# The weights' low part read last in each step of a split-precision encoder block

## The chip, the core and the metric

One NeuronCore of a Trainium2 chip runs the whole block as one program. The metric is the device time of one execution in microseconds (us), as the median of several executions. PE is the matrix engine, PEld the loading of its stationary operand, DVE the vector engine, ACT the scalar engine, POOL and SP the two that mostly issue transfers.

## The reference

The block works on `x` of 256 tokens by 2048 channels, in float32. It is a gated feed-forward layer at half weight, then two token mixers side by side (band attention and retention, each with its own gate), then a second gated feed-forward layer, and a final normalisation:

```python
x = x + 0.5 * swiglu_ffn(rmsnorm(x, g1), w1_gate, w1_up, w1_down)
proj = rmsnorm(x, gm) @ w_in                 # 2048 -> 11264 channels
branch_a = chunked_band_attention(...) @ w_out_att
branch_r = (silu(g_r) * chunkwise_retention(...)) @ w_out_ret
merged = sigmoid(gate_a) * branch_a + sigmoid(gate_r) * branch_r
x = x + merged @ w_out
x = x + 0.5 * swiglu_ffn(rmsnorm(x, g2), w2_gate, w2_up, w2_down)
return rmsnorm(x, gf)
# swiglu_ffn(x, wg, wu, wd) = (silu(x @ wg) * (x @ wu)) @ wd, inner width 5632
```

Nearly all of the time goes into products of the 256 rows with weight matrices that are read once.

## The kernel before, in words

**Split products.** Every float32 operand of a large product is held as two tiles of a shorter type: a high part, and a low part that holds the rest. Activations have `ahi` and `alo`, weights `whi` and `wlo`. A product of 128 rows by 128 depths by 512 columns is the sum of three matmuls into one PSUM bank, in `three` (L126): `ahi`·`whi` at L131, `ahi`·`wlo` at L132, `alo`·`whi` at L133. The activation is PE's stationary operand (128x128, loaded on PEld before every matmul) and the weights are the moving operand (128x512).

**Steps.** The program is a list of steps. A step handles one weight tile of 256 depths by 512 columns (`KC` = 2 blocks of 128 depths). A standard step (`standard`, L135) multiplies it with both halves of the 256 tokens, each into a bank of its own (`acc` 0 and 1), so it is 2 x 2 x 3 = 12 matmuls. Its job, a `Gemm`, has 8, 4 or 2 steps for 16, 8 or 4 blocks of depth; 24 jobs have 8 steps, 40 have 4, and 24 have 2, which is 400 standard steps, 176 of them the first or last of their job. A step of a `Strassen` group, which computes two weight matrices at once with seven products in place of eight, multiplies one 256x512 tile with one set of activations: 2 x 3 = 6 matmuls into one bank. There are 23 groups of 28 steps. `weave` mixes standard steps between the pairs of steps of a group.

**What makes the weights ready.** SP issues the transfer of the raw tile (`raw`, five buffers). `split` (L119) makes the two parts: ACT casts `raw` into `hi` (L123) and DVE then subtracts, `lo` = `raw` - `hi` (L124). In a group some of the tiles are sums of weights instead, made on DVE from two kept tiles `z..k` and `z..x` (L538 subtracts, L551 adds); their parts are named `hiz..` and `loz..`. There are four buffers each for `hi` and for `lo`. `prep_upto` lets the preparation of a step's tiles stand up to three steps ahead of its products in the order of ACT and DVE. ACT and DVE also take the sums out of PSUM (for instance L606, L739 and L742 on ACT, L706 on DVE), so the splits stand in line with that work.

**Order.** Each engine works through its instructions in the order in which the program is written out; nothing reorders them. So PE waits at the first matmul that reads a tile until that tile is there. A buffer of `hi` or `lo` is taken again when the last matmul that reads it has ended.

Of the kernel before, what the change touches and what calls it, by code (L numbers as in the profile page):

```python
# [27 lines left out]
KC = 2  # L28
# [44 lines left out]
def block_kernel(ctx: ExitStack, tc: tile.TileContext, x, g1, w1g, w1u, w1d, gm, w_in, rel, woa, wor, wo,  # L73
                 g2, w2g, w2u, w2d, gf, cos, sin, decay, ident, out):
    nc = tc.nc
# [33 lines left out]
    def weights_tile(name):  # L109
        return wpool.tile([P, KC, NB], F32, tag="raw", bufs=RAW_BUFS, name=name)  # L110

    def chunk(w, r0, c0):
        return w[r0 : r0 + KC * P, c0 : c0 + NB].rearrange("(k p) n -> p k n", p=P)

    def fetch(t, w, r0, c0, parts=(slice(0, KC),)):
        for p in parts:
            nc.sync.dma_start(t[:, p, :], chunk(w, r0, c0)[:, p, :])

    def split(raw, name, parts=(slice(0, KC),)):  # L119
        hi = wpool.tile([P, KC, NB], F32R, tag="hi", bufs=SPLIT_BUFS, name=f"hi{name}")  # L120
        lo = wpool.tile([P, KC, NB], F32R, tag="lo", bufs=SPLIT_BUFS, name=f"lo{name}")
        for p in parts:
            nc.scalar.copy(hi[:, p, :], raw[:, p, :])  # L123
            nc.vector.tensor_sub(lo[:, p, :], raw[:, p, :], hi[:, p, :].bitcast(F32))  # L124
        return hi, lo

    def three(acc, a, w, first, last, read_between=False):

        (ahi, alo), (whi, wlo) = a, w
        more = {"skip_group_check": True} if read_between else {}  # L130
        nc.tensor.matmul(acc, ahi, whi, start=first, stop=False, **more)  # L131
        nc.tensor.matmul(acc, ahi, wlo, start=False, stop=False, **more)  # L132
        nc.tensor.matmul(acc, alo, whi, start=False, stop=last, **more)  # L133

    def standard(job, k0):  # L135

        made = {}
        c = len(steps)

        parts = [slice(j, j + 1) for j in range(KC)] if c == 0 else [slice(0, KC)]  # L140

        def load():
            made["raw"] = weights_tile(f"raw{c}")
            fetch(made["raw"], job.w, job.rows[k0], job.col0, parts)

        def prep():
            made["hl"] = split(made.pop("raw"), c, parts)

        def products(only=None):
            if k0 == 0 and only in (None, 0) and not job.seed:  # L150
                open_banks(job)
            hi, lo = made["hl"]
            for part, (t, cs) in enumerate(job.parts):
                for j in range(KC):
                    k = k0 + j
                    if only in (None, part):
                        three(
                            job.acc[part], job.act(k, t), (hi[:, j, cs], lo[:, j, cs]),
                            k == 0 and not job.seed, k == job.nk - 1, bool(job.seed),
                        )  # L160
            if only is None and k0 + KC == job.nk:
                close(job)

        return Step(job, k0, load, prep, ("raw",), products)

    def close(job):

        follow = job.next if job.next is not None and job.next.seed else None

        def begin(t):  # L170
            follow.acc.append(acc_tile(f"acc{len(done)}_{t}", follow.tags[t]))
            follow.seed(follow.acc[t], t)
            done.append(follow)

        if follow is not None:
            follow.acc = []
            begin(0)
        if job.evict is None:
            job.done(job.acc)
        else:  # L180
            job.evict(job.acc[0], 0)
        if follow is not None:
            begin(1)
        if job.evict is not None:
            job.evict(job.acc[1], 1)

    def open_banks(job):
        job.acc = [acc_tile(f"acc{len(done)}_{t}", job.tags[t]) for t in range(NT)]
        job.acc += [side_tile(f"acc{len(done)}_{t}") for t in range(NT, len(job.parts))]
        job.acc = [a[:, : cs.stop - cs.start] for a, (t, cs) in zip(job.acc, job.parts)]  # L190
        done.append(job)
# [289 lines left out]
    class Strassen:  # L481
# [43 lines left out]
        def step(self, phase, jc, of_sum):  # L525
            made = {}
            name = f"{self.name}{phase}{jc}{'rs'[of_sum]}"
            n = HALF_K // KC

            def load():  # L530
                made["raw"] = weights_tile(f"raw{name}")
                i = 2 - phase
                fetch(made["raw"], self.w[i], self.rows(1, jc), self.col[i])

            def third():

                x, k = self.x[jc], self.kept[jc]
                nc.vector.tensor_sub(k, x, k)  # L538
                nc.gpsimd.dma_start(x, chunk(self.w[0], self.rows(1, jc), self.col[0]), accum_op=ALU.add)

            def prep():
                x = self.x[jc]
                if not of_sum:
                    if phase == 0:
                        made["w"] = split(self.kept[jc], name)
                        self.first(jc)
                        return
                    raw = made.pop("raw")
                    made["w"] = split(raw, name)
                    if phase == 1:  # L550
                        nc.vector.tensor_add(x, x, raw)  # L551
                elif phase == 2:
                    made["w"] = split(self.kept.pop(jc), name)
                elif phase == 3:
                    made["w"] = split(self.x.pop(jc), name)
                else:
                    made["w"] = split(x, name)
                    if phase == 1:
                        third()

            bank, form, fresh, closing = {
# [4 lines left out]
            }[phase, of_sum]  # L566

            def products():
                hi, lo = made["w"]
                if fresh and jc == 0:  # L570
                    self.bank(bank)
                for i in range(KC):
                    three(
                        self.acc[bank], self.norm.form(form, KC * jc + i), (hi[:, i, :], lo[:, i, :]),
                        fresh and jc == 0 and i == 0, closing and jc == n - 1 and i == KC - 1, True,
                    )
                if jc == n - 1:
                    self.end(phase, of_sum)

            loaded = not of_sum and phase in (1, 2)  # L580
            frees = ["raw"] if loaded else ["kept"] if of_sum and phase > 1 else []
            return Step(self, 0, load if loaded else None, prep, frees, products)

        def end(self, phase, of_sum):
# [647 lines left out]
```

## Time and profile before

| | |
|---|---|
| median of 3 runs | 2102.69 us (2100.75 to 2103.42) |
| the profiled execution | 2103.97 us, of it the span 2102.2 us |
| PE | 2064.1 us busy, 9256 matmuls and transposes |
| PEld | 1687.6 us busy |
| DVE | 1760.9 us busy |
| ACT | 1407.8 us busy |
| granted PE clock | 0.998 of full speed |
| read from memory | 462.65 MB, 224 GB/s over the span |

The profile is of one execution, with times in us from the span's start. In its rows stand the start, the duration, the engine, the line, and what is written from what; in brackets how long the engine was idle before and what ended that. A matmul's duration there is longer than its spacing, since one begins while the last is still draining; so the distance from start to start is what counts.

### The profile page before, as it was taken

To read this page: it belongs to the slowest core of one execution; us is meant where nothing else is said; L and a number is where in the kernel's file an instruction comes from. 1 tells how busy PE (TensorE), PEld (TensorE's weight loads), DVE (VectorE), ACT (ScalarE), POOL (GpSimd) and SP (SyncE) were. 2 spreads that over 40 slices of the span, in tenths; PEclk is the share of its full clock that TensorE was granted. 3 is DMA by queue.
4 is the path that set the end of the run, shared out by engine and by line. 5 is a ranking of instruction groups with operands and counts; after the bars stand their busy time and mean duration, and the time that the engine had idled before them with its cause. 6 is when DMAs were issued, how large, how long until landed. Compare 5 with 4: busy or idle time off the path is not lost.

```text
span 2102.2 us, 25815 instructions
## 1 busy us (share of the span) xinstructions
PE 2064.1 (98%) x9256; PEld 1687.6 (80%) x9256; DVE 1760.9 (84%) x1823; ACT 1407.8 (67%) x1734; POOL 274.0 (13%) x322
## 2 busy tenths in 40 slices
PE   9999999999999999999999999999999999999998
PEld 7788878878887888878788888887888788888886
DVE  7998889888997799889966667568889988898986
ACT  7677667767777766767664434556777677677785
POOL 1111211122111110122100000010122012110200
PEclk9999999999999999999999999999999999999999
DMA  8767886788668777788775645575788678866873
GB/s 302 210 214 229 261 229 198 233 253 253 192 227 247 241 209 235 256 280 250 217 256 178 220 131 191 189 245 167 229 271 238 184 228 261 245 195 225 277 210 130
DMA packets 219025, 473.27 MB, mean 225 GB/s; under 512 B 14784, under 2 KB 15536, under 8 KB 218896
## 3 DMA queue, kind: packets, MB, share of 16 engines
q1 hardware_dynamic: 161088, 310.42, 44.0%
q0 software_dynamic: 54752, 155.88, 27.4%
q10 hardware_dynamic: 3056, 5.32, 0.7%
q8 instruction: 72, 1.18, 0.2%
q14 instruction: 57, 0.47, 0.1%
HBM read 462.65 MB, written 8.91 MB: 224 GB/s over the span
## 4 chain that ended last, share of the span: by engine, by line
PE 76%; DVE 11%; issue 4%; ACT 4%; DMA 3%; POOL 0%; ACTq 0%; POOLq 0%; DVEq 0%
PE acc L132 15%; PE acc L133 14%; PE acc L131 14%; DVE lo L124 2%; DMA raw<-in_ffn_w_down_dram 2%; ACT hi L123 1%; DMA raw<-in_w_in_dram 1%; DMA rawz91523r<-in_ffn_w_up_dram 1%; DMA z992x<-in_ffn_w_gate_dram 1%; PE z128a L132 0%; PE z800a L132 0%; PE z380a L131 0%; PE z128a L131 0%; PE z800a L131 0%; PE z380a L133 0%
## 5 line engine op out<-in xcount | busy, mean ns | idle before, releaser
L124 DVE TENSOR_TENSOR lo<-raw,hi 128x1024 fp32r<-128x1024 f32 (+1 forms) x401 | 487.4, 1218 | 173.4 <-ACT hi L123 171.6
L123 ACT CAST hi<-raw 128x1024 fp32r<-128x1024 f32 (+1 forms) x401 | 419.0, 1048 | 231.3 <-PE acc L133 143.0
L739 ACT ACTIVATE acc<-xall 128x512 f32<-128x512 f32 x96 | 57.5, 599 | 8.4 <-DVE f1g L706 3.5
L742 ACT ACTIVATE xall<-acc 128x512 f32<-128x512 f32 x96 | 56.4, 588 | 4.6 <-PE acc L133 3.9
L131 PE MATMUL acc<-hi,mgh 128*128 128x512 f32 x128 | 50.1, 392 | 0.0
L133 PE MATMUL acc<-hi,mgl 128*128 128x512 f32 x128 | 49.8, 389 | 0.0
L132 PE MATMUL acc<-lo,mgh 128*128 128x512 f32 x128 | 49.8, 389 | 0.0
L132 PE MATMUL acc<-lo,nma01h 128*128 128x512 f32 x96 | 38.0, 396 | 2.7 <-DVE lo L124 2.7
L131 PE MATMUL acc<-hi,nma01h 128*128 128x512 f32 x96 | 38.6, 402 | 0.0
L131 PE MATMUL acc<-hi,nma00h 128*128 128x512 f32 x96 | 38.5, 401 | 0.0
L132 PE MATMUL acc<-lo,nma00h 128*128 128x512 f32 x96 | 37.9, 395 | 0.3 <-DVE lo L124 0.3
L133 PE MATMUL acc<-hi,nma01l 128*128 128x512 f32 x96 | 37.5, 391 | 0.0
L133 PE MATMUL acc<-hi,nma00l 128*128 128x512 f32 x96 | 37.5, 391 | 0.0
L131 PE MATMUL acc<-hi,nma10h 128*128 128x512 f32 x96 | 37.5, 390 | 0.0
L131 PE MATMUL acc<-hi,nma11h 128*128 128x512 f32 x96 | 37.4, 390 | 0.0
L133 PE MATMUL acc<-hi,nma11l 128*128 128x512 f32 x96 | 37.4, 390 | 0.0
L133 PE MATMUL acc<-hi,nma10l 128*128 128x512 f32 x96 | 37.4, 390 | 0.0
L132 PE MATMUL acc<-lo,nma10h 128*128 128x512 f32 x96 | 37.4, 389 | 0.0
L132 PE MATMUL acc<-lo,nma11h 128*128 128x512 f32 x96 | 37.4, 389 | 0.0
L133 PEld LDWEIGHTS acc<-hi,mgl 128*128 128x128 f32 x128 | 24.0, 188 | 4.9
L131 PEld LDWEIGHTS acc<-hi,mgh 128*128 128x128 f32 x128 | 24.0, 188 | 4.9
L132 PEld LDWEIGHTS acc<-lo,mgh 128*128 128x128 f32 x128 | 24.0, 188 | 4.9
(6130 smaller groups left out, 7143.7 us busy)
## 6 DMA issues: line engine op xcount, KB each, us to landing
raw<-in_ffn_w_down_dram SPq DMA_DIRECT2D x176, 512.0 KB, 6.3
raw<-in_w_in_dram SPq DMA_DIRECT2D x96, 512.0 KB, 4.5
raw<-in_ffn_w_up_dram SPq DMA_DIRECT2D x32, 512.0 KB, 9.8
raw<-in_w_out_dram SPq DMA_DIRECT2D x32, 512.0 KB, 3.7
raw<-in_ffn_w_gate_dram SPq DMA_DIRECT2D x31, 512.0 KB, 4.8
raw<-in_w_out_att_dram SPq DMA_DIRECT2D x16, 512.0 KB, 3.9
raw<-in_w_out_ret_dram SPq DMA_DIRECT2D x16, 512.0 KB, 4.1
z380x<-in_w_in_dram POOLq DMA_DIRECT2D x8, 512.0 KB, 8.0
```

The costliest lines, as they stand in the source:

```text
L123: nc.scalar.copy(hi[:, p, :], raw[:, p, :])
L124: nc.vector.tensor_sub(lo[:, p, :], raw[:, p, :], hi[:, p, :].bitcast(F32))
L131: nc.tensor.matmul(acc, ahi, whi, start=first, stop=False, **more)
L132: nc.tensor.matmul(acc, ahi, wlo, start=False, stop=False, **more)
L133: nc.tensor.matmul(acc, alo, whi, start=False, stop=last, **more)
L739: nc.scalar.activation(acc, xs[t][:, cols], AF.Copy, scale=2.0)
L742: nc.scalar.activation(xs[t][:, cols], acc, AF.Copy, scale=0.5)
```

## The change

In a step, all the matmuls that read the high part of the weights are issued first, and those with the low part after them. For each block of depth, `ahi`·`whi` (L132 of the changed kernel) is followed by `alo`·`whi` (L133); only then come the matmuls `ahi`·`wlo` (L135). In a step of a group that is four matmuls and then two. In a standard step inside its job both halves of the tokens are taken together, eight matmuls and then four; in the first and the last step of a job each half is done by itself, four and two, and then again four and two, as before one half after the other. The same matmuls are done, into the same banks, with the same operands.

```diff
-    def three(acc, a, w, first, last, read_between=False):
-        (ahi, alo), (whi, wlo) = a, w
+    def three(products, read_between=False):
         more = {"skip_group_check": True} if read_between else {}
-        nc.tensor.matmul(acc, ahi, whi, start=first, stop=False, **more)
-        nc.tensor.matmul(acc, ahi, wlo, start=False, stop=False, **more)
-        nc.tensor.matmul(acc, alo, whi, start=False, stop=last, **more)
+        for acc, (ahi, alo), (whi, _), first, _ in products:
+            nc.tensor.matmul(acc, ahi, whi, start=first, stop=False, **more)
+            nc.tensor.matmul(acc, alo, whi, start=False, stop=False, **more)
+        for acc, (ahi, _), (_, wlo), _, last in products:
+            nc.tensor.matmul(acc, ahi, wlo, start=False, stop=last, **more)
...
+            turns = [
+                [
+                    (
+                        job.acc[part], job.act(k0 + j, t), (hi[:, j, cs], lo[:, j, cs]),
+                        k0 + j == 0 and not job.seed, k0 + j == job.nk - 1,
+                    )
+                    for j in range(KC)
+                ]
+                for part, (t, cs) in enumerate(job.parts) if only in (None, part)
+            ]
+
+            if 0 < k0 < job.nk - KC:
+                turns = [sum(turns, [])]
+            for products in turns:
+                three(products, bool(job.seed))
...
-                for i in range(KC):
-                    three(
+                three([
+                    (
                         self.acc[bank], self.norm.form(form, KC * jc + i), (hi[:, i, :], lo[:, i, :]),
-                        fresh and jc == 0 and i == 0, closing and jc == n - 1 and i == KC - 1, True,
+                        fresh and jc == 0 and i == 0, closing and jc == n - 1 and i == KC - 1,
                     )
+                    for i in range(KC)
+                ], True)
```

The first place is PE's order in the first feed-forward layer, around 290 us. Before, it has a standard step inside its job (tile `hi_2492`, `lo_2493`, sums `acc`), of which the first half and the start of the second are shown, and the group step on tile `z12813s`:

```order
L131 MATMUL acc_0_2461<-hi_2492,f1a1h_1730 128x512 [waits Activation_49]
L132 MATMUL acc_0_2461<-lo_2493,f1a1h_1730 128x512 [waits DVE_49]
L133 MATMUL acc_0_2461<-hi_2492,f1a1l_1731 128x512
...
L131 MATMUL acc_1_2465<-hi_2492,f1a1h_1730 128x512
...
L131 MATMUL z128a<-hiz12813s,n1s6h 128x512 [waits Activation_49]
L132 MATMUL z128a<-loz12813s,n1s6h 128x512 [waits DVE_49]
L133 MATMUL z128a<-hiz12813s,n1s6l 128x512
```

In the same place of the changed kernel stand these; between the rows shown, the pair L132 and L133 comes a second time for the second block of depth:

```order
L132 MATMUL acc_0_2461<-hi_2492,f1a1h_1730 128x512 [waits Activation_49]
L133 MATMUL acc_0_2461<-hi_2492,f1a1l_1731 128x512
...
L132 MATMUL acc_1_2465<-hi_2492,f1a1h_1730 128x512
L133 MATMUL acc_1_2465<-hi_2492,f1a1l_1731 128x512
...
L135 MATMUL acc_0_2461<-lo_2493,f1a1h_1730 128x512 [waits DVE_49]
...
L135 MATMUL acc_1_2465<-lo_2493,f1a1h_1730 128x512 x2
...
L132 MATMUL z128a<-hiz12813s,n1s6h 128x512 [waits Activation_49]
L133 MATMUL z128a<-hiz12813s,n1s6l 128x512
...
L135 MATMUL z128a<-loz12813s,n1s6h 128x512 [waits DVE_49]
```

PE's wait for DVE moved from the second matmul of the step to the ninth in the standard step, and from the second to the fifth in the group step.

The second place is DVE's order at the same point. Before, the subtractions L124 that make the low parts wait for ACT's cast and, where the tile came from memory, for its transfer:

```order
L124 TENSOR_TENSOR loz12812s<-z128x_2158,hiz12812s 128x1024 [waits DVE_49,Activation_49]
L538 TENSOR_TENSOR z128k_2146<-z128x_2158,z128k_2146 128x1024
L124 TENSOR_TENSOR loz12813s<-z128x_2191,hiz12813s 128x1024 [waits Activation_49]
L538 TENSOR_TENSOR z128k_2173<-z128x_2191,z128k_2173 128x1024
L124 TENSOR_TENSOR lo_2551<-raw_2404,hi_2550 128x1024 [waits DMAHW6_49,Activation_49]
```

In the changed kernel:

```order
L124 TENSOR_TENSOR loz12812s<-z128x_2158,hiz12812s 128x1024 [waits DVE_49,PE_49,Activation_49]
L547 TENSOR_TENSOR z128k_2146<-z128x_2158,z128k_2146 128x1024
L124 TENSOR_TENSOR loz12813s<-z128x_2191,hiz12813s 128x1024 [waits PE_49,Activation_49]
L547 TENSOR_TENSOR z128k_2173<-z128x_2191,z128k_2173 128x1024
L124 TENSOR_TENSOR lo_2551<-raw_2404,hi_2550 128x1024 [waits DMAHW6_49,PE_49,Activation_49]
```

The order on DVE is the same (L547 is L538 of before), and so is that of ACT, SP and POOL; 876 instructions of DVE have another set of waits, for the most part with PE added.

More of the change, by code (lines that the diff above doesn't have):

```diff
@@ L152, in products @@
             hi, lo = made["hl"]
[L153 to L156, printed above, removed]
-                        three(
-                            job.acc[part], job.act(k, t), (hi[:, j, cs], lo[:, j, cs]),
-                            k == 0 and not job.seed, k == job.nk - 1, bool(job.seed),
-                        )
+            turns = [
[12 more added lines that the diff above has]
+                three(products, bool(job.seed))
             if only is None and k0 + KC == job.nk:
@@ L571, in products @@
                     self.bank(bank)
-                for i in range(KC):
-                    three(
+                three([
+                    (
                         self.acc[bank], self.norm.form(form, KC * jc + i), (hi[:, i, :], lo[:, i, :]),
-                        fresh and jc == 0 and i == 0, closing and jc == n - 1 and i == KC - 1, True,
+                        fresh and jc == 0 and i == 0, closing and jc == n - 1 and i == KC - 1,
                     )
+                    for i in range(KC)
+                ], True)
                 if jc == n - 1:
```

## The prediction

> **What bounds the kernel now.** The page comes first, for the share of each engine.
>
> ```profile
> span 2102.2 us, 25815 instructions
> PE 2064.1 (98%) x9256; PEld 1687.6 (80%) x9256; DVE 1760.9 (84%) x1823; ACT 1407.8 (67%) x1734; POOL 274.0 (13%) x322
> ```
>
> PE is busy for 98% of the span. A pure reordering of its matmuls can win only time in which it stands still, so the question is how much that is and who causes it. First its pace where nothing disturbs it, from the timeline of PE between 307 and 310 us:
>
> ```profile
> 307.35 0.39 PE L131 MATMUL z128b<-hiz12822r,n1a01h 128*128 128x512 f32 x1
> ...
> 308.48 0.39 PE L133 MATMUL z128b<-hiz12822r,n1a01l 128*128 128x512 f32 x1
> 308.70 0.39 PE L131 MATMUL z128a<-hiz12821s,n1s7h 128*128 128x512 f32 x1
> ...
> 310.06 0.39 PE L131 MATMUL z128b<-hiz12823r,n1a01h 128*128 128x512 f32 x1
> ```
>
> From the first to the last row are twelve matmuls (two group steps of six): 2.71 / 12 = 0.226 us each. The middle pair is a change of bank (`b` to `a`): 0.22, no dearer than the rest.
>
> Next the view of waits, for the lines that touch the split of the weights (us in total, times, longest):
>
> ```profile
> DVE lo L124 <- ACT hi L123: 171.6, 142, 2.9
> ACT hi L123 <- PE acc L133: 143.0, 86, 3.5
> PEld acc L132 <- DVE lo L124: 33.2, 67, 1.1
> PE acc L132 <- DVE lo L124: 10.3, 21, 0.8
> ...
> PEld acc L131 <- ACT hi L123: 2.0, 3, 0.9
> ...
> PEld z915a L132 <- DVE loz91523s L124: 0.7, 1, 0.7
> PEld z684c L132 <- DVE loz68413r L124: 0.7, 1, 0.7
> PEld z12c L132 <- DVE loz1213r L124: 0.7, 1, 0.7
> PEld z800a L132 <- DVE loz80013s L124: 0.6, 1, 0.6
> PEld z128a L132 <- DVE loz12813s L124: 0.6, 1, 0.6
> ...
> PEld z531c L132 <- DVE loz53100s L124: 0.3, 1, 0.3
> PEld z761a L132 <- DVE loz76101r L124: 0.2, 1, 0.2
> ```
>
> In standard steps PE's loads waited 67 times for a low part of the weights, 33.2 us in all. The seven group rows add 0.7 x 3 + 0.6 x 2 + 0.3 + 0.2 = 3.8 us, so 74 waits and 37.0 us. For the high part it waited three times, 2.0 us. The low part is what comes late, and L132, the second matmul of a step, is where it is met.
>
> A wait on PEld isn't all lost by PE, which still streams the matmul before. Two of the waits in the timeline give the difference:
>
> ```profile
> 188.27 0.39 PE L131 MATMUL acc<-hi,f1a9h 128*128 128x512 f32 x1
> ...
> 188.96 0.19 PEld L132 LDWEIGHTS acc<-lo,f1a9h 128*128 128x128 f32 x1 [0.72 <-DVE lo L124]
> ...
> 189.29 0.39 PE L133 MATMUL acc<-hi,f1a9l 128*128 128x512 f32 x1
> ```
>
> ```profile
> 290.26 0.39 PE L131 MATMUL acc<-hi,f1a1h 128*128 128x512 f32 x1
> 291.03 0.50 PE L132 MATMUL acc<-lo,f1a1h 128*128 128x512 f32 x1 [0.38 <-DVE lo L124]
> 291.36 0.39 PE L133 MATMUL acc<-hi,f1a1l 128*128 128x512 f32 x1
> 291.59 0.40 PE L131 MATMUL acc<-hi,f1a1h 128*128 128x512 f32 x1
> 291.83 0.40 PE L132 MATMUL acc<-lo,f1a1h 128*128 128x512 f32 x1
> ```
>
> ```profile
> 291.03 0.19 PEld L132 LDWEIGHTS acc<-lo,f1a1h 128*128 128x128 f32 x1 [0.81 <-DVE lo L124]
> ```
>
> L131 to L133 should take 2 x 0.226 = 0.45. It took 1.02 with a wait of 0.72, and 1.10 with a wait of 0.81: lost are 0.57 and 0.65, each the wait less some 0.155. Over 74 waits the loss is 37.0 - 74 x 0.155 = **25.5 us**. About 0.10 of each loss lies behind the wait: L132 to L133 took 0.33, since the next load could not run ahead. And the matmuls after it come 0.23 and 0.24 apart, not 0.226.
>
> Why is the low part late? The timelines of ACT and DVE around the next two waits:
>
> ```profile
> 289.95 1.05 ACT L123 CAST hiz12813s<-z128x 128x1024 fp32r<-128x1024 f32 x1 [0.96 <-DVE z128x L551]
> 290.90 1.04 ACT L123 CAST hi<-raw 128x1024 fp32r<-128x1024 f32 x1
> ```
>
> ```profile
> 294.36 1.22 DVE L124 TENSOR_TENSOR loz12813s<-z128x,hiz12813s 128x1024 fp32r<-128x1024 f32 x1
> 295.49 1.22 DVE L538 TENSOR_TENSOR z128k<-z128x,z128k 128x1024 f32<-128x1024 f32 x1
> 296.63 1.22 DVE L124 TENSOR_TENSOR lo<-raw,hi 128x1024 fp32r<-128x1024 f32 x1
> ```
>
> ```profile
> 295.03 0.39 PE L131 MATMUL z128a<-hiz12813s,n1s6h 128*128 128x512 f32 x1
> ...
> 295.97 0.39 PE L133 MATMUL z128a<-hiz12813s,n1s6l 128*128 128x512 f32 x1
> ...
> 296.89 0.40 PE L131 MATMUL acc<-hi,f1a2h 128*128 128x512 f32 x1
> ...
> 298.24 0.39 PE L133 MATMUL acc<-hi,f1a2l 128*128 128x512 f32 x1
> ```
>
> The high part of the tile used at 296.89 was done at 291.94; its low part ended at 297.85. DVE stands in a queue of its own, one operation every 1.13 us, while the high parts lie ready for five microseconds.
>
> **The change part by part.**
>
> *The wait moves.* The low part is first read by the ninth matmul of a standard step inside a job (second before): 7 x 0.226 = 1.58 us later. In group steps and in the first and last step of a job it is the fifth: 3 x 0.226 = 0.68 later. The longest wait, 1.1, means a loss of some 0.95. So in an inner step every single loss is covered by matmuls on the high part, which is there; in the others those up to 0.68 are.
>
> *What is left.* Where waits follow each other in one busy stretch of DVE, the time not lost at the first comes back at the second. Around 290 us the losses are 0.65 (inner step), 295.97 - 295.03 - 0.45 = 0.49 (group step) and 298.24 - 296.89 - 0.45 = 0.90 (inner step). After the change the first is covered; PE reaches the group step 0.65 earlier, where 0.65 + 0.49 = 1.14 meets a cover of 0.68, so 0.46 is lost, and 0.10 with the late load; the third then has 1.14 + 0.90 - 0.56 = 1.48 against 1.58 and is covered. Of 2.04, 0.56 stays. The second layer has the same pair of places (`z800a`), so 1.1 for both. The long waits that fall into first or last steps (176 of 400 standard steps) keep 0.95 - 0.68 + 0.10, some 0.4 each; of three of those I make 1.2. Together 2.3 stay, and **23.2 go**.
>
> *The slower pace behind late loads.* The waits' disappearance returns matmuls from 0.23 and more to 0.226. With 0.005 for twelve matmuls behind each of 74 waits it is up to 4.4 us; with nothing, 0. I take half, **2.2**.
>
> *The casts.* `hi` is now last read by the eighth of twelve matmuls (the fourth of six), so its buffer is free 4 x 0.226 = 0.90 (0.45) earlier for ACT, which waited 143.0 us for PE. This makes high parts earlier still. I count nothing: its cover, PE being behind ACT, is what remains.
>
> *The new wait on DVE.* L124 now waits for PE's last matmul of the step four tiles back as well. Queued behind it on DVE are the next sums (L538, L551), splits and evictions, and PE waits for those. Before, the cast waited for that step's last matmul, and L124 for the cast:
>
> ```profile
> L123 ACT CAST hi<-raw 128x1024 fp32r<-128x1024 f32 (+1 forms) x401 | 419.0, 1048 | 231.3 <-PE acc L133 143.0
> ```
>
> So L124 could not start until 1.05 us behind it; now it can start 0.45 to 0.90 sooner, never later. The price is that of more entries in DVE's queue:
>
> ```profile
> L124 DVEq EVENT_SEMAPHORE  x836: 21/21/2085, 8.1 to 2082.5; - x168
> ```
>
> At worst 876 new ones at 0.021 would be 18.4 us of DVE time. I take zero: L124 and L538 above start 1.13 us apart though each lasts 1.22, with such entries between, so DVE takes them while it still works on the last operation. The Trainium skill, "Perfetto Trace Analysis", section "Identifying Dependency Chains", says that an instruction that waits for several engines may get extra semaphore instructions ahead of it, which speaks against this change; the 836 rows agree that they exist, and by that rule with no hiding, the 18.4 us would take back most of the gain.
>
> *Sum.* 2103.97 - 23.2 - 2.2 = 2078.6 for the profiled execution, which is 1.3 above the median of the runs; I forecast **2078** for a median.
>
> **The rivals.**
>
> *Half comes back (DVE is the bound).* If DVE's busy stretches hold PE anyway, the time saved is lost at the next thing DVE gives, as around 295 us, or in its evictions. For it speaks a stretch with many waits:
>
> ```profile
> 100.00:300.00 200.00, 198.48 (x883) 162.04 (x882) 183.11 (x168) 139.68 (x157) 31.37 (x35) 1.00 0.75 229
> ```
>
> DVE is busy there for 183.11 of 200. Against it: DVE itself stood 171.6 us for casts, so its stretches end, and start again when PE frees buffers. Half of 25.5 gives 2103.97 - 12.7 = 2091.
>
> *The change does nothing.* If what is late is the whole preparation, PE would stop at the high part instead, for as long: 2102.7. For it only the three waits on `hi`, 2.0 us; the rows at 290.90 and 296.63 say the contrary.
>
> *Slower: the change of banks.* Inner steps (24 jobs x 6 and 40 x 2, 224) now change bank three times inside the step instead of once: 448 changes more. If each exposes a load as a late one does, 0.10, it is 45 us: 2103.97 - 25.4 + 45 = 2124. It decides from 25.4 / 448 = 0.057 per change on. Against it: the pair at 308.48 and 308.70 above, and likewise every old step's change of bank. The Trainium skill, "TensorE: Matmul & The Clock Gate", section "A second HAM failure mode: psum-queue depth-cycling", tells of a kernel that cycled through PSUM banks and kept falling back to the slow clock; the granted clock is 1.00 in the window above, with a bank change every six matmuls already, so no run here shows it.
>
> **How the numbers follow.** Forecast 0.74; half comes back 0.14; nothing 0.07; slower 0.05. Less than 0.2%, about 4 us, could not be told from no change here, so the first two are faster, 0.88. The range: at the low end all of the 25.5 and 4.4 go, and the median lies 1.3 under the profiled run, 2072.8, to which I add a little for waits on evictions that shrink too, 2071; at the high end the rival of half, 2091, and the unknown price on DVE, 2094. That leaves the last two cases out.
>
> **What would show it.** Right: waits on L124 in the PEld rows fall from 37 us to under 6 us, at L135 and mostly in group steps; the matmul pace stays 0.226; ACT's wait for PE shrinks. Wrong: the waits move to `hi` at L132 or to transposes and evictions (DVE bound); or the pace at a change of bank rises above 0.23 (slower).

## The result, and the profile after

The changed kernel takes 2080.23 us (median of 4 runs, 2078.51 to 2083.68) against 2103.06 before: a ratio of 0.9891, 95% interval 0.9879 to 0.9902, or 22.8 us less. The profiled execution took 2078.51, with a span of 2076.4.

The head of its page:

```profile
span 2076.4 us, 26151 instructions
PE 2048.9 (99%) x9256; PEld 1692.5 (82%) x9256; DVE 1756.2 (85%) x1823; ACT 1404.3 (68%) x1734; POOL 273.7 (13%) x322
```

ACT and DVE are busy for as long as before, to 5 us, and PE does the same 9256 instructions; the span is shorter by what PE stood still. The busy time of PE hides most of that, since a row of 0.39 that comes 0.226 after the last covers short gaps, so the standstill is added up from the starts of PE's rows. There are 8593 pairs of matmuls on weights that follow each other directly. What lies over 0.226 between their starts is 48.5 us before and 23.2 after, 25.3 less, where the span is 25.8 shorter. The parts, rounded:

| us over 0.226 from start to start | before | after |
|---|---|---|
| at a matmul whose load waited for a low part, and at the one behind it | 27.0 | 2.0 |
| the same for a high part | 0.7 | 2.6 |
| the same for ACT's copies out of a group's bank | 5.6 | 5.3 |
| up to 0.28 from start to start, with no such wait | 8.1 | 6.0 |
| the rest | 7.2 | 7.3 |

In the view of waits, the lines that answer to those shown of before (L132 is now the first matmul of a pair, L135 the one on the low part, L359 the old L350):

```profile
DVE lo L124 <- ACT hi L123: 182.9, 143, 3.7
ACT hi L123 <- PE acc L133: 148.1, 94, 3.0
...
PEld acc L132 <- ACT hi L123: 3.5, 5, 1.4
...
PEld f1a9p L359 <- DVE f1g L717: 3.0, 2, 2.8
PEld acc L135 <- DVE lo L124: 1.9, 4, 0.5
...
PEld z531b L135 <- DVE loz53123r L124: 0.5, 1, 0.5
...
PEld z12a L135 <- DVE loz1213s L124: 0.3, 1, 0.3
PEld z684b L135 <- DVE loz68423r L124: 0.3, 1, 0.3
PEld z684a L135 <- DVE loz68413s L124: 0.3, 1, 0.3
PEld z800a L135 <- DVE loz80013s L124: 0.2, 1, 0.2
```

The loads' waits for a low part, on which the first row rests, went from 37.0 us in 74 to 1.9 + 0.5 + 0.9 + 0.2 = 3.5 us in 9. The waits for the high part grew a little, from 2.0 to 3.5.

The same place as in the prediction, the inner step that lost 0.65 and the two group steps after it, on PE after the change:

```profile
285.92 0.39 PE L132 MATMUL acc<-hi,f1a1h 128*128 128x512 f32 x1
...
286.60 0.39 PE L133 MATMUL acc<-hi,f1a1l 128*128 128x512 f32 x1
286.83 0.39 PE L132 MATMUL acc<-hi,f1a1h 128*128 128x512 f32 x1
...
287.74 1.07 PE L135 MATMUL acc<-lo,f1a1h 128*128 128x512 f32 x4
288.64 0.39 PE L132 MATMUL z128a<-hiz12812s,n1s6h 128*128 128x512 f32 x1
...
290.00 0.39 PE L132 MATMUL z128a<-hiz12813s,n1s6h 128*128 128x512 f32 x1
...
290.92 0.63 PE L135 MATMUL z128a<-loz12813s,n1s6h 128*128 128x512 f32 x2
291.38 0.39 PE L132 MATMUL acc<-hi,f1a2h 128*128 128x512 f32 x1
```

and on DVE there:

```profile
287.18 1.22 DVE L124 TENSOR_TENSOR loz12812s<-z128x,hiz12812s 128x1024 fp32r<-128x1024 f32 x1
288.31 1.22 DVE L547 TENSOR_TENSOR z128k<-z128x,z128k 128x1024 f32<-128x1024 f32 x1
289.44 1.22 DVE L124 TENSOR_TENSOR loz12813s<-z128x,hiz12813s 128x1024 fp32r<-128x1024 f32 x1
290.58 1.22 DVE L547 TENSOR_TENSOR z128k<-z128x,z128k 128x1024 f32<-128x1024 f32 x1
```

From 285.92 to 291.38 PE does 24 matmuls in 5.46 us; before, the same 24 took from 290.26 to 296.89, 6.63. Saved are 1.17, and the two losses that the prediction read there were 0.65 + 0.49. The low part `loz12813s` is done at 290.66 and first read at 290.92: DVE is as busy as before, but now PE has other work until then. The third and the fourth of the rows (286.60 and 286.83) are a change of bank inside the step, 0.23 apart; the four matmuls from 287.74, with another change among them, take 0.90 / 4 = 0.225 each.

### The profile page after: what moved, and what is told of

Read it like the earlier page. It is cut to its first block, busy times and chain, and to the rows that moved or that the text cites. A ratio compares the mean times of both kernels' runs of the same rounds, so it can differ in the third digit from the quotient of the medians.

```text
span 2076.4 us, 26151 instructions
## 1 busy us (share of the span) xinstructions
PE 2048.9 (99%) x9256; PEld 1692.5 (82%) x9256; DVE 1756.2 (85%) x1823; ACT 1404.3 (68%) x1734; POOL 273.7 (13%) x322
## 4 chain that ended last, share of the span: by engine, by line
PE 92%; DVE 2%; DMA 2%; ACT 2%; issue 1%; ACTq 0%; POOLq 0%; DVEq 0%; POOL 0%
PE acc L132 17%; PE acc L135 17%; PE acc L133 17%; DMA raw<-in_ffn_w_down_dram 1%; DMA rawz53123r<-in_w_in_dram 1%; DVE lo L124 1%; ACT hi L123 0%; PE z128a L132 0%; PE z12a L135 0%; PE z128a L135 0%; PE z128a L133 0%; PE z12a L132 0%; PE z915a L135 0%; PE z418a L135 0%; PE z761a L132 0%
## 5 line engine op out<-in xcount | busy, mean ns | idle before, releaser
L124 DVE TENSOR_TENSOR lo<-raw,hi 128x1024 fp32r<-128x1024 f32 (+1 forms) x401 | 488.4, 1221 | 186.2 <-ACT hi L123 182.9
L123 ACT CAST hi<-raw 128x1024 fp32r<-128x1024 f32 (+1 forms) x401 | 418.7, 1048 | 231.1 <-PE acc L133 148.1
L132 PE MATMUL acc<-hi,mgh 128*128 128x512 f32 x128 | 50.2, 392 | 0.0
L133 PE MATMUL acc<-hi,mgl 128*128 128x512 f32 x128 | 49.8, 389 | 0.0
L132 PE MATMUL acc<-hi,nma00h 128*128 128x512 f32 x96 | 38.5, 401 | 0.0
L132 PE MATMUL acc<-hi,nma01h 128*128 128x512 f32 x96 | 38.4, 400 | 0.0
L133 PE MATMUL acc<-hi,nma00l 128*128 128x512 f32 x96 | 37.4, 390 | 0.0
L132 PE MATMUL acc<-hi,nma10h 128*128 128x512 f32 x96 | 37.4, 390 | 0.0
L133 PE MATMUL acc<-hi,nma01l 128*128 128x512 f32 x96 | 37.4, 390 | 0.0
L133 PE MATMUL acc<-hi,nma11l 128*128 128x512 f32 x96 | 37.4, 390 | 0.0
L133 PE MATMUL acc<-hi,nma10l 128*128 128x512 f32 x96 | 37.4, 389 | 0.0
L132 PE MATMUL acc<-hi,nma11h 128*128 128x512 f32 x96 | 37.4, 389 | 0.0
L135 PE MATMUL acc<-lo,mgh 128*128 128x512 f32 x128 | 35.5, 389 | 0.0
L135 PE MATMUL acc<-lo,nma11h 128*128 128x512 f32 x96 | 29.6, 390 | 0.0
L135 PE MATMUL acc<-lo,nma00h 128*128 128x512 f32 x96 | 29.6, 389 | 0.0
L135 PE MATMUL acc<-lo,nma01h 128*128 128x512 f32 x96 | 29.6, 389 | 0.0
L135 PE MATMUL acc<-lo,nma10h 128*128 128x512 f32 x96 | 29.6, 389 | 0.0
L135 PEld LDWEIGHTS acc<-lo,mgh 128*128 128x128 f32 x128 | 24.0, 188 | 5.0
L133 PEld LDWEIGHTS acc<-hi,mgl 128*128 128x128 f32 x128 | 24.0, 188 | 4.9
L132 PEld LDWEIGHTS acc<-hi,mgh 128*128 128x128 f32 x128 | 24.0, 188 | 4.8
```

The source lines that it names most:

```text
L133: nc.tensor.matmul(acc, alo, whi, start=False, stop=False, **more)
L135: nc.tensor.matmul(acc, ahi, wlo, start=False, stop=last, **more)
```

## The experiments

The theory was that of **cover**: the low part is late by DVE's queue, and PE loses only what the matmuls on the high part ahead of it don't cover. The rival that had to be told from it is the **early buffer**: the change also lets go of the high part's buffer sooner, so ACT casts and DVE subtracts sooner. A third is the **pace**: the mere sequence of matmuls. The times are medians; the ratio is to the kernel before on the same chip.

**e1: the low part first.** In `three` of the kernel before:

```diff
-        nc.tensor.matmul(acc, ahi, whi, start=first, stop=False, **more)
-        nc.tensor.matmul(acc, ahi, wlo, start=False, stop=False, **more)
+        nc.tensor.matmul(acc, ahi, wlo, start=first, stop=False, **more)
+        nc.tensor.matmul(acc, ahi, whi, start=False, stop=False, **more)
```

> Order of before, but each product begins with the matmul on the low part, so PE meets the low part one matmul (0.226 us) earlier than before. Theory of cover (the low part is late by fixed amounts, and PE loses what the matmuls on the high part ahead of it don't cover): each of the 74 waits grows by 0.226 and a few new ones appear, some 10 to 20 us more than before, 2113 to 2123. Theory of the early buffer (what the change won is that the buffers of the high part come free sooner for ACT): the high part is read last by the last matmul as before, so no change, 2103 within 3. Theory of the pace (the sequence of operands on PE is what matters): nothing definite, every triple is only permuted, 2103 within 3.

2112.1 us, ratio 1.0042 (1.0029 to 1.0054): 8.8 slower. One matmul less of cover costs, a little under the range named (10 to 20). The high part's buffer is held as before, so the early buffer has no part in this.

**e2: the low part third.** Again in the kernel before:

```diff
-        nc.tensor.matmul(acc, ahi, wlo, start=False, stop=False, **more)
-        nc.tensor.matmul(acc, alo, whi, start=False, stop=last, **more)
+        nc.tensor.matmul(acc, alo, whi, start=False, stop=False, **more)
+        nc.tensor.matmul(acc, ahi, wlo, start=False, stop=last, **more)
```

> Order of before, but in each product the matmul on the low part is third and not second, so there is one more matmul of cover (0.226 us) and nothing else: the buffer of the high part is read last by the matmul before the last of its step. Theory of cover: with the 74 losses of before, 0.34 on the mean, cut by up to 0.226 each, 9 to 13 us less than before, 2090 to 2094. Theory of the early buffer: it comes one matmul sooner (against four or two in the change), at most a third of the gain, 2095 to 2101.

2089.64 us, 0.9937 (0.9924 to 0.9949): 13.6 faster, just over the range of cover and beyond that of the early buffer. Swapping two lines is worth over half of the whole change. Since the high part's buffer comes free one matmul sooner as well, the 13.6 are not cover alone. The waits on the loads, which are met at L133 there:

```profile
PEld acc L133 <- DVE lo L124: 18.6, 44, 1.0
```

**e3: the halves one after the other.** The changed kernel without the joining of both halves in inner steps:

```diff
-            if 0 < k0 < job.nk - KC:
-                turns = [sum(turns, [])]
```

> The changed kernel, but a standard step inside its job does the two halves of the tokens one after the other, as its first and last steps do: the low part is met at the fifth matmul everywhere (cover 0.68 instead of 1.58 in inner steps) and the high part's buffer is free after the tenth matmul and not the eighth. Theory of cover: the losses over 0.68, ten or so of up to 0.95, come back with 0.1 for the late load each: 4 to 7 us over the changed kernel, 2084 to 2087. Theory of the early buffer: half of the lead of 0.90 is lost in inner steps, so a third to half of the gain, 2088 to 2092.

2083.53 us, 0.9904 (0.9891 to 0.9918): 3.3 over the changed kernel, a little under what cover expected and clear of the other. The intervals of the two ratios overlap, so the 3.3 by itself is not clear of noise; the waits are. Its loads wait 7.5 us in 12 on low parts in standard steps, against 1.9 in 4:

```profile
PEld acc L135 <- DVE lo L124: 7.5, 12, 1.0
```

**e4: no cover, but the buffer free early.** In the changed kernel:

```diff
-        for acc, (ahi, alo), (whi, _), first, _ in products:
+        for i, (acc, (ahi, alo), (whi, wlo), first, _) in enumerate(products):
             nc.tensor.matmul(acc, ahi, whi, start=first, stop=False, **more)
+            if i == 0:
+                nc.tensor.matmul(acc, ahi, wlo, start=False, stop=False, **more)
             nc.tensor.matmul(acc, alo, whi, start=False, stop=False, **more)
-        for acc, (ahi, _), (_, wlo), _, last in products:
+        for acc, (ahi, _), (_, wlo), _, last in products[1:]:
```

> The changed kernel, but the first matmul on the low part stands second in each turn, as before the change; the others stay at the end. So there is no more cover than before, but the buffer of the high part comes free after the ninth of twelve matmuls in inner steps (after the fifth of six in groups). Theory of cover: the losses of before return, 2100 to 2104. Theory of the early buffer: most of the gain stays, 2080 to 2090.

2093.43 us, 0.9949 (0.9935 to 0.9962): 9.9 faster. Neither expectation held: cover alone said no gain, the early buffer alone most of it. Two more kernels took it apart.

**e5: cover, but the buffer held.** The changed kernel, with the last `alo`·`whi` of each turn moved to its very end:

```diff
-        for acc, (ahi, alo), (whi, _), first, _ in products:
+        end = len(products) - 1
+        for i, (acc, (ahi, alo), (whi, _), first, _) in enumerate(products):
             nc.tensor.matmul(acc, ahi, whi, start=first, stop=False, **more)
-            nc.tensor.matmul(acc, alo, whi, start=False, stop=False, **more)
-        for acc, (ahi, _), (_, wlo), _, last in products:
-            nc.tensor.matmul(acc, ahi, wlo, start=False, stop=last, **more)
+            if i < end:
+                nc.tensor.matmul(acc, alo, whi, start=False, stop=False, **more)
+        for i, (acc, (ahi, alo), (whi, wlo), _, last) in enumerate(products):
+            nc.tensor.matmul(acc, ahi, wlo, start=False, stop=last and i < end, **more)
+            if i == end:
+                nc.tensor.matmul(acc, alo, whi, start=False, stop=last, **more)
```

> The changed kernel, but the last matmul of the low activations on the high part of the weights is put at the very end of each turn, so the high part's buffer is held as long as before the change, and the cover is one matmul shorter (1.36 us in inner steps, 0.45 in groups and in first and last steps). Theory of cover: 2 to 4 us over the changed kernel, 2081 to 2084. Theory of the early buffer: the gain is gone, 2098 to 2103.

2084.93 us, 0.9912 (0.9898 to 0.9925). With the buffer held as long as before the change and one matmul less of cover, 17.8 of the gain stay, which cover alone brings. It is 4.7 over the changed kernel, where cover alone expected 2 to 4; the intervals of the two ratios overlap a little, though every run of e5 lies above every run of the change.

**e9: neither.** The kernel e4 with the edit of e5: the first low part second, the buffer held to the end of the turn. In a turn of two products, so in groups and in the first and last steps of a job, that is the very order of before; only inner steps, 224 of 12 matmuls, have another. The diff is to e5, without the head of its first loop.

```diff
+            if i == 0:
+                nc.tensor.matmul(acc, ahi, wlo, start=False, stop=False, **more)
             if i < end:
                 nc.tensor.matmul(acc, alo, whi, start=False, stop=False, **more)
         for i, (acc, (ahi, alo), (whi, wlo), _, last) in enumerate(products):
-            nc.tensor.matmul(acc, ahi, wlo, start=False, stop=last and i < end, **more)
+            if i > 0:
+                nc.tensor.matmul(acc, ahi, wlo, start=False, stop=last and i < end, **more)
```

> The kernel in which the first matmul on the low part stands second in each turn and the others at the end, with one edit: the last matmul of the low activations on the high part of the weights is put at the very end of the turn. So neither the cover is longer than before the change nor the high part's buffer free earlier; only the sequence of the rest is new. It tells what the 10 us of the kernel without that edit came from. Theory of the early buffer (besides the cover, ACT casts and so DVE subtracts sooner, which is what won there): the gain is gone, 2101 to 2105. If the sequence itself wins (PE's pace, or the matmuls on the low part grouped at the end): the 10 us stay, 2092 to 2096.

2103.67 us, 1.0001 (0.9992 to 1.0010). The gain of e4 is gone, to within 2 us, though the inner steps have another order than before. So the order of an inner step wins nothing by its pace (that of the groups is tried in e7), and e4, which differs from e9 only in where the last `alo`·`whi` of a turn stands, won by its early buffer. The four kernels side by side:

| | buffer held as before | buffer free early |
|---|---|---|
| low part second, as before | e9: 2103.67 | e4: 2093.43 |
| low part late | e5: 2084.93 | the change: 2080.23 |

How the early buffer wins is seen at one step of the first layer (the one that multiplies the activations `f1a9`), on PE in e9 and then in e4, where L135 and L134 are the matmul on the low part that stands second:

```profile
131.03 0.39 PE L133 MATMUL acc<-hi,f1a9h 128*128 128x512 f32 x1
131.43 0.50 PE L135 MATMUL acc<-lo,f1a9h 128*128 128x512 f32 x1
```

```profile
131.21 0.39 PE L132 MATMUL acc<-hi,f1a9h 128*128 128x512 f32 x1
131.44 0.39 PE L134 MATMUL acc<-lo,f1a9h 128*128 128x512 f32 x1
```

and the subtraction that makes this low part, on DVE in e9 and then in e4:

```profile
130.15 1.22 DVE L124 TENSOR_TENSOR lo<-raw,hi 128x1024 fp32r<-128x1024 f32 x1
```

```profile
129.70 1.22 DVE L124 TENSOR_TENSOR lo<-raw,hi 128x1024 fp32r<-128x1024 f32 x1
```

In e9 it ends at 131.37, 0.34 after the step's first matmul, and PE waits. In e4 it ends at 130.92, 0.29 before it. DVE runs ahead by 0.63 more, about the three matmuls (0.68) by which ACT got its buffer sooner in inner steps. Where that began is seen on ACT, at a cast that had waited for an inner step to let go of its buffer, in e9 and then in e4:

```profile
111.25 1.05 ACT L123 CAST hiz1233s<-z12x 128x1024 fp32r<-128x1024 f32 x1 [1.09 <-PE acc L142]
```

```profile
110.80 1.06 ACT L123 CAST hiz1233s<-z12x 128x1024 fp32r<-128x1024 f32 x1 [0.41 <-PE acc L135]
```

The 0.45 between the two is handed on to DVE, whose subtraction for the tile `z5100r` starts at 115.80 and at 115.35; from there it works without a stop up to those at 130.15 and 129.70. Only about one tile in five has so large a shift: over the first 1040 of the 1044 weight tiles, counted from the first matmul of each step, both parts are ready sooner in e4, the high part by 0.23 on the mean and the low part by 0.20. Over the program, the waits in standard steps:

```profile
PEld acc L135 <- DVE lo L124: 32.6, 64, 1.1
```

```profile
PEld acc L134 <- DVE lo L124: 25.8, 53, 1.1
```

The first is e9, the second e4. From start to start on PE, as in the table above, low parts cost 27.1 in e9 and 21.3 in e4, which is 5.8 of the 9.8 by which the whole falls; the rest is spread over high parts, pace and what remains.

**e7 and e8: one kind of step alone.** With `old_three`, a function that has the order of before, in place of `three`; e7 puts it into the standard steps, where the joining of both halves goes too, and e8 into the groups; of each edit only the call is shown:

```diff
-                three(products, bool(job.seed))
+                old_three(products, bool(job.seed))
```

```diff
-                three([
+                old_three([
```

> The new order in the steps of the groups alone; standard steps have the order of before. Theory of cover: the seven waits in groups, 3.8 us on the loads, go, and what they held up is met again at the next standard step for a part: 0 to 4 us less than before, 2099 to 2103. If the gain came from the pace of matmuls in general, groups, with 3864 of 8676 matmuls, should bring four tenths of it: 2093.

> The new order in the standard steps alone; groups have the order of before. Theory of cover: the 67 waits in standard steps go, and PE, now earlier, loses a little more in the group steps that follow in the same busy stretch of DVE: 18 to 21 us less than before, 2082 to 2085. By the pace of matmuls in general: six tenths of the gain, 2089.

e7: 2102.88 us, 0.9999 (0.9989 to 1.0009). e8: 2079.6 us, 0.9888 (0.9873 to 0.9903). All of the gain lies in the standard steps, more of it than cover expected (18 to 21), and the edit in the groups is worth nothing that can be measured. In e7, the waits in standard steps are as large as before, 35.3 us in 62, so what the group steps no longer lost was probably lost at the next standard step, as in the prediction's reckoning of carried losses. The order of the groups, which has no gain here, wins nothing by its pace either.

**e6: all steps joined.** The changed kernel with `turns = [sum(turns, [])]` in the first and last steps too:

```diff
-            if 0 < k0 < job.nk - KC:
-                turns = [sum(turns, [])]
+            turns = [sum(turns, [])]
```

> The changed kernel, but first and last steps of a job take both halves of the tokens together too, as inner steps do. Theory of cover: the cover grows from 0.68 to 1.58 in 174 steps where little is lost any more, at most 1 us gained; against it the second bank is used two matmuls sooner in a first step and the first bank is complete five matmuls later in a last step, so evictions start up to 1.1 us later, which a following job's first step may wait for: 2079 to 2086, no better than the changed kernel by more than 1.

2081.28 us, 0.9899 (0.9884 to 0.9915): no different from the change. Waits of a kind that the change hasn't appear, for a bank that is wanted two matmuls sooner:

```profile
PEld acc L132 <- ACT f2g L706: 1.2, 1, 1.2
PEld acc L132 <- ACT acc L749: 1.2, 3, 0.4
```

**e10: a standard step between.** The list of what PE still waits for after the change has five lines of this kind, two of which are

```profile
PEld z800a L132 <- ACT z800c L617: 1.2, 1, 1.2
PEld z877a L132 <- ACT z877c L617: 1.2, 1, 1.2
```

In five groups the last step of the third phase stands right before the first of the fourth, in the same bank, which ACT must copy out in between. `weave` is made to set a standard step there always:

```diff
-                if credit >= (0.2 if (i + 1) % (HALF_K // KC) == 0 else 0.6) and next_standard():
+                if credit >= (-1.0 if i + 1 == 3 * (HALF_K // KC) else 0.2 if (i + 1) % (HALF_K // KC) == 0 else 0.6) and next_standard():
```

> The changed kernel, but a standard step is always set between the last group step of the third phase and the first of the fourth. In five of the 23 groups none stands there, and PE waits for ACT to copy the sum (L617), 1.2 us each on the loads and some 0.95 us of PE's time. Theory that what is left of PE's standstill is made of such single waits: up to 4.7 us less than the changed kernel, 2075 to 2078. If DVE's queue is the bound by now: PE waits elsewhere for as long, 2079 to 2082.

2075.43 us, 0.9873 (0.9859 to 0.9887), 4.8 less than the changed kernel's median and within the first range; all of its runs lie below all of the change's, and none of the five lines is left. It is the fastest version here. What PE's loads wait for in it:

```profile
PEld acc L132 <- ACT hi L123: 3.7, 5, 1.1
PEld f1a9p L359 <- DVE f1g L717: 3.0, 2, 2.7
PEld acc L135 <- DVE lo L124: 2.6, 6, 0.5
PEld psb L336 <- ACT bias L341: 2.0, 1, 2.0
```

## Why the prediction was right, and where not

The time, 2078 foreseen and 2080.23 measured, lies well inside the range; for the profiled execution the sum gave 2078.6, and it took 2078.51. The main mechanism, cover, is shown by e1 and e5. But so close an agreement hides two misses that cancel, which is luck: more went at the low parts than was reckoned, and the high parts, which the sum leaves out, cost more.

- *The loss of 25.5 us from the low parts.* It was there. The table has 27.0 before, 0.36 for each of the 74 waits, and 2.0 after, where 2.3 were to stay: 25.0 went, and not 23.2.
- *The cover.* The more matmuls on the high part stand ahead of the low one, the less is lost: 2112, 2103, 2090, 2084, 2080 for none, one, two, four everywhere, and eight in inner steps. In e2, e3 and the change the buffer comes free sooner as well, so the clean proof is e1 (8.8 more) and e5 (17.8 less), in which it is held as before.
- *The casts, "I count nothing".* This is the step that failed. The early buffer is worth 10.2 by itself (e9 to e4). In the change it adds less, since cover has taken most of what it could save: e5 to the change is 4.7, of which cover for one matmul was put at 2 to 4. The prediction saw that high parts would come earlier, but held that they were early enough. The link stands in its own words on the rival of half: DVE's stretches of work start again when PE frees buffers. A stretch that begins with an earlier cast runs earlier as a whole, relative to PE, with everything in DVE's queue. The sign that it named, a shorter wait of ACT for PE, did not come: in the rows above it grew from 143.0 to 148.1, and from e9 to e4, where the buffer is all that differs, from 144.4 to 157.2. That total does not measure how early the casts are.
- *What is left at the group step at 295 us.* Foreseen were 0.46 and 0.10. Nothing is lost there: the low part was there 0.26 before it was read. That too is the early buffer, as e5 shows, which holds it:

```profile
294.00 1.22 DVE L124 TENSOR_TENSOR loz12813s<-z128x,hiz12813s 128x1024 fp32r<-128x1024 f32 x1
```

```profile
294.44 0.39 PE L133 MATMUL z128a<-hiz12813s,n1s6h 128*128 128x512 f32 x1
295.28 0.73 PE L137 MATMUL z128a<-loz12813s,n1s6h 128*128 128x512 f32 x2 [0.45 <-DVE loz12813s L124]
```

In e5 the subtraction starts 4.09 after the first matmul of the inner step (289.91), as before (4.10), and 0.61 is lost, of which one more matmul of cover would leave 0.38, close to the 0.46. After the change it starts 3.52 after that matmul. The 2.0 that stay lie at other places than reckoned, so that the total fits is luck as well.
- *The slower pace behind late loads, 2.2.* The short distances without a wait add up to 8.1 before and 6.0 after, so 2.1 went. The size was half of an upper bound, taken without a row that shows it; that it fits is luck.
- *The high parts.* The prediction has no term for them. They cost 1.9 more than before (0.7 to 2.6), which takes back the 1.8 that the low parts gave beyond the 23.2.
- *The new wait on DVE, at zero.* Right. The entries on L124 rose from 836 to 1155. Where DVE goes on without idle after a whole subtraction of L124, the next operation starts 1.136 us after it before (median of 756) and 1.135 after (of 814). The row:

```profile
L124 DVEq EVENT_SEMAPHORE  x1155: 21/50/2885, 8.0 to 2056.6; - x193
```

- *The rivals.* Half coming back: no. PE's loads wait 1.5 us more on the high part and 1.2 on `f1g`, and DVE's share of the chain that ended last, before and then after, fell:

```profile
PE 76%; DVE 11%; issue 4%; ACT 4%; DMA 3%; POOL 0%; ACTq 0%; POOLq 0%; DVEq 0%
PE 92%; DVE 2%; DMA 2%; ACT 2%; issue 1%; ACTq 0%; POOLq 0%; DVEq 0%; POOL 0%
```

The change of banks: no price, 0.23 at 286.83 and the four at 0.225; and e9, whose inner steps change bank three times as those of the change do, is at 1.0001. No fall of the clock shows: the granted clock of the profiled run is 0.999.

What the trace does not settle is how the 4.7 between e5 and the change splits, over the whole program, between one matmul of cover and the buffer, since that edit moves both.

## What to carry to other kernels

When an engine in order reads two operands of which one is always made later, read everything that needs the early one first; one swapped pair of lines brought over half of it here. Ask of every such reordering also when each buffer is read for the last time, since the engine that refills it may head the queue that was late. A gain that is reckoned from one mechanism and comes out right in its sum is no proof of that mechanism alone: a two by two of kernels showed the second.

## What the runs showed of the hardware

No price of the order of matmuls on PE shows as long as nothing is waited for. e9 keeps the cover and the buffers of before and has another order in its 224 inner steps, with three changes of bank in each and not one, and it takes the same time to 0.1% (1.0001); so does e7, with another order in the groups (0.9999).

A load that comes late costs the next matmul too: the 74 matmuls whose loads waited for a low part began 19.8 us late in all, and those right behind them another 7.2, some 0.10 each.

A wait of DVE that is met already costs nothing that shows, although its row became longer in the middle (21 ns before, 50 after): with 319 rows more on L124, the work still starts every 1.13 to 1.14 us.
